# Attention's output products issued in halves of a weight block, each half behind one head's values; the first chunk's first two k tiles with their low-row products last

## The chip, the cores and the metric

The kernel runs on one core of a Trainium2 chip. The metric is device time in microseconds (us) of one execution; the median of several executions is compared. TensorE (PE) does the matmuls, and its weight loads are listed apart as PEld. VectorE (DVE), ScalarE (ACT) and GpSimd (POOL) do the rest, and SyncE (SP) issues most transfers. Each engine works through its own instructions in the order that was fixed when the kernel was built.

## The reference

Two layers over 256 rows of 1024 channels, each of the form half a SwiGLU feed-forward, a mixer, half a second feed-forward. The mixer of layer 0 is a convolution module, that of layer 1 is multi-head latent attention with 8 heads. What the change touches is the end of the attention and the start of a feed-forward:

```python
s = (q_nope . k_nope + q_rope . k_rope) * scale      # per head, 2 blocks of 128 queries, chunk-causal mask
p = softmax(s)
o = p . v                                            # per head, 128 channels
h = h + concat(o over 8 heads) @ w_o                 # (256 x 1024) @ (1024 x 1024)
h = h + 0.5 * (silu(n @ w1) * (n @ w3)) @ w2         # n = RMSNorm(h), w1 and w3 (1024 x 2816)
```

Everything is float32 in the inputs and the output.

## The kernel before, in words

**Three products for one.** A float32 matrix is split in a high part (a cast to fp32r) and a low part (what the cast left). `mm3` (line 271) makes one product of three matmuls into the same PSUM tile: high rows by low weights (the page's line 273), high rows by high weights (276), low rows by high weights (277). The rows' two parts are Xh and Xl for a feed-forward and Oh and Ol for the attention's outputs; the weights' are `hi` and `lo`. `some` (279) makes a chosen subset of the three, named by the letters l, h and x in that order.

**Weights.** The weights come as blocks of 128 x 2048 in a fixed list (`blocks`). `load_to` (209) issues a block's transfer into one of 3 `raw` buffers (SP's queue), casts the high part on ACT (line 187) and subtracts on DVE (line 188), each in 2 pieces, into one of 5 pairs of buffers. `weights` (213) takes the next block for use and calls `load_ahead`. A cast is ordered behind the last 6 urgent instructions of its engine that were written down before it (`behind`, 141).

**The order.** The build (line 1503) has a planner that simulates a timeline and gives every engine a fixed order: of the instructions that its simulation holds ready, the one of the highest priority goes next. Priority is the place in the program, except for functions wrapped in `urgent` (193), which go ahead. `order` (137) adds a constraint between two instructions without a wait of its own. The planner's order can therefore differ from the program's: work written later is pulled forward where the engine would otherwise stand idle in the simulation.

**Attention's heads** (lines 1289 to 1374). For a head, `scores` (1294) makes the two score tiles in one PSUM bank of tag B (of 3), `softmax` (1306) takes the maxima on DVE, the powers on ACT (1315) and the scaling on DVE (1320); `probs` (1324) transposes the three 128 x 128 blocks into another bank of tag B (tp, line 317) and copies them on ACT (1327, `ptT`); `values` (1334) multiplies with V into the only bank of tag C (pv, 1336 and 1337), and `evicted` (1330) writes Oh on ACT (1331) and Ol on DVE (1332). A head's values wait for the bank until the head before has been evicted. Only heads 3 to 6 have an urgent eviction. The loop over i (1358) writes scores of head i, transposes of head i - 2 and values of head i - 3. The scores of heads 0 to 2 and the last projection (nope) stand ahead of it.

**The output products** are kept by `Rows` (563): four accumulators of 128 x 512 (two blocks of 128 rows `tb`, two halves of the channels `d`). A weight block of `wo` covers two heads (k tiles f = 2i and 2i + 1), so `block(i)` (577) issues 4 accumulators x 2 heads x 3 = 24 matmuls. Blocks 0 and 1 are written after the values of heads 3 and 5 (i = 6 and 8, line 1369); `finish` (584) writes blocks 2 and 3, accumulator by accumulator, adds each to h as it completes and starts the next norm: `early` (392) transposes block 0 of the new rows on PE and splits it into Xh and Xl, `begin` (404) turns block 1 on DVE and by transfers through DRAM (ht, hd, hb), and `end` (414) splits that.

**The feed-forward's first chunk** (`first_chunk`, 642) runs in five stretches of k tiles: gate weights on row block 0 (k 0 to 7), up weights on row block 0 (k 0 to 3), gate on row block 1 (k 0 to 7), then the rest. It is used by the two feed-forwards whose second row block is turned by transfers, which are layer 1's: one starts at 459.59 us of the trace and one, behind the attention, at 730.15 us.

Of the kernel before, what the change touches and what calls it, by code (L numbers as in the profile page):

```python
# [19 lines left out]
P = 128  # L20
D = 1024
S = 256
NT = S // P
KT = D // P
# [10 lines left out]
VH = 128  # L35
# [7 lines left out]
PIECES = 2  # L43
# [41 lines left out]
def trunk(ctx: ExitStack, tc: tile.TileContext, x, xt, first, pos, invf, gfin, wdw,  # L85
          f1w13, f1w2, f2w13, f2w2, cw1, cw2, wa, wuq, wukv, wo, wpair, out):
    nc = tc.nc
# [45 lines left out]
    n_used = [0]  # L133
# [3 lines left out]
    def order(ins, first):  # L137
        tc.add_manual_dep(ins.ins, first.name, mybir.DependencyInfo(
            mybir.DependencyClass.NoSync, mybir.DependencyReason.DATA), reason="order")
# [7 lines left out]
    casts = {}  # L147
# [58 lines left out]
    def load_ahead(ahead=W_BUFS - 2):  # L206
        load_to(min(len(blocks), n_used[0] + ahead))
# [5 lines left out]
    def weights(n=1, more=True):  # L213
        out = []
        for _ in range(n):
            n_used[0] += 1
            if more:
                load_ahead()
            else:
                load_ahead(0)  # L220
            out.append(loaded[n_used[0] - 1])
        return out
# [19 lines left out]
    for k in range(KT):  # L242
        c = slice(k % 4 * 512, k % 4 * 512 + 512)
# [27 lines left out]
    def mm3(o, ah, al, bh, bl, start, stop, after=()):  # L271

        mm = nc.tensor.matmul(o, ah, bl, start=start, stop=False)  # L273
        for a in after:
            order(mm, a.ins)
        nc.tensor.matmul(o, ah, bh, start=False, stop=False)  # L276
        return nc.tensor.matmul(o, al, bh, start=False, stop=stop)  # L277

    def some(o, kinds, ah, al, bh, bl, start, stop):

        for n, kind in enumerate(kinds):
            mm = nc.tensor.matmul(o, al if kind == "x" else ah, bl if kind == "l" else bh,  # L282
                                  start=start and n == 0, stop=stop and n == len(kinds) - 1)
        return mm

    def tbs(tb):
        return slice(tb * P, (tb + 1) * P)
# [275 lines left out]
    class Rows:  # L563
# [10 lines left out]
                         f == f1 - 1, [*after, *after_last] if j else after)  # L574
            return mm

        def block(self, i):
            part, = weights()
            for tb in range(NT):
                for d in range(2):  # L580
                    apart = self.last and (tb, d) == (1, 1)
                    self.mm(part, i, tb, d, self.o[tb, d], 0, self.nk - (4 if apart else 0))

        def finish(self, rh, make_next, act):
            nb = self.nk // 2
# [44 lines left out]
    def ffn_in(act, X, make_next, beside):  # L630
# [11 lines left out]
        def first_chunk(X, u):  # L642

            kn = HB // 512
            parts = weights(3, False)
            X.begin()
            parts += weights(1, False)
            for m in range(2):
                for tb in range(NT):
                    u[m, tb] = bank("A", "u")  # L650
            last = None
            for n, (m, tb, ks) in enumerate(((0, 0, range(8)), (1, 0, range(4)), (0, 1, range(8)), (1, 0, range(4, 8)),
                                             (1, 1, range(8)))):
                if n == 2:
                    X.late()
                elif n == 3:
                    load_ahead()
                for k in ks:
                    hi, lo = parts[2 * m + k // kn]
                    c = slice(k % kn * 512, k % kn * 512 + 512)  # L660
                    mm = mm3(u[m, tb], X.xh[:, k, tbs(tb)], X.xl[:, k, tbs(tb)], hi[:, c], lo[:, c], k == 0,
                             k == KT - 1, (last,) if last is not None and k == ks[0] else ())
                last = mm

        for c in range(6):
# [476 lines left out]
    def mla_in(act, X, make_next, cc, sn):  # L1142
# [146 lines left out]
        Oh = act.tile([P, H, S], F32R, tag="Oh", name="Oh")  # L1289
        Ol = act.tile([P, H, S], F32R, tag="CQ", name="Ol")  # L1290

        score_last, maxima, powers, scaled = [], [], [], []

        def scores(hd):
# [29 lines left out]
        def probs(pr):  # L1324
            b = transposed(pr, 0, 3)
            pt = act.tile([P, 3 * P], F32, tag="ptT", name=uid("ptT"), bufs=2)
            nc.scalar.copy(pt, b[:, :3 * P])
            return pt

        def evicted(hd, b):  # L1330
# [3 lines left out]
        def values(hd, pt):  # L1334
            b = bank("C", "pv")
            nc.tensor.matmul(b[:, :S], VV[:, 0, hd * VH:(hd + 1) * VH], pt[:, :S], start=True, stop=False)
            nc.tensor.matmul(b[:, P:S], VV[:, 1, hd * VH:(hd + 1) * VH], pt[:, S:], start=False, stop=True)

            (urgent if hd in (3, 4, 5, 6) else lambda f: f)(evicted)(hd, b)

        pr, pt = {}, {}
        part, = weights(1, False)
        load_ahead(1)

        table = urgent(nc.scalar.activation)(small.tile([P, 1], F32, tag="silu", name="exp"), neghalf, AF.Exp)
        order(table, kept.ins)
# [11 lines left out]
        for i in range(2, H + 3):  # L1358
            if 2 < i < H:
                pr[i] = scores(i)  # L1360
            if i == 6:
                load_ahead(5)
            if i in (3, 4):
                load_ahead(i - 1 + (i == 4))
            if i - 2 < H:
                pt[i - 2] = probs(pr[i - 2])
            if i - 3 in pt:
                values(i - 3, pt[i - 3])
            if i in (6, 8):
                o.block((i - 6) // 2)  # L1370

            if i in (8, 9):
                load_to(n_used[0] + i - 4)
# [141 lines left out]
```

## Time and profile before

| what | us |
|---|---|
| median of 3 runs (lowest to highest) | 919.18 (918.69 to 919.48) |
| the profiled execution | 918.68 |
| its span, first to last instruction | 916.9 |
| PE busy in the span | 908.9 |
| DVE, ACT, POOL busy | 591.1, 492.8, 127.6 |
| granted TensorE clock, mean | 0.999 |

The profile's page gives busy time by engine, then groups of instructions by source line. Beside it there are lists of who waited for whom, groups by tile, sums over stretches of time, and a timeline by engine; in a timeline each row has its start, its length, its engine, its line, the operation, the tiles (out<-in) and how many were merged, and in square brackets the idle time of the engine before it. A PE row's length is longer than the distance to the next start, because matmuls overlap; the distance between two starts is the time that a matmul takes of the engine.

### The profile page before, as it was taken

Reading aid. Unit: us, or ns where it says so; the run is one execution under the profiler, and the core shown is the slowest. Engines: PE = TensorE matmul, PEld = TensorE weight load, DVE = VectorE, ACT = ScalarE, POOL = GpSimd, SP = SyncE. Lnnn points to the kernel's source line nnn. Section 1 sums busy time; section 2 is a strip of 40 time slices with the busy share of each in tenths; the row PEclk is TensorE's granted clock in tenths of the full one; section 3 lists DMA queues with packets and bytes.
Section 4 is the critical chain, followed back from the end, with each engine's and each line's share of the span. In section 5 each row is a group of like instructions: output and inputs, shape, how many; then the busy total and the mean of one; then the engine's idle time right before and its main releaser. Section 6 shows DMA issues by size and latency. Waiting matters only on the chain.

```text
span 916.9 us, 12085 instructions
## 1 busy us (share of the span) xinstructions
PE 908.9 (99%) x4337; PEld 764.6 (83%) x4337; DVE 591.1 (64%) x931; ACT 492.8 (54%) x842; POOL 127.6 (14%) x261
## 2 busy tenths in 40 slices
PE   9999999999999999999999999999999999999997
PEld 7888888898988888888888888888898888888886
DVE  6886764489987666655476665545768676566533
ACT  7654454388877444543364544443677574454422
POOL 1720000079951000000010000001400000000000
PEclk9999999999999999999999999999999999999999
DMA  9987776533227667766567777754445478776711
GB/s 339 321 294 248 277 253 222 188 139 138 93 85 270 243 233 239 251 222 226 184 203 271 260 244 239 239 203 132 168 143 184 149 258 277 250 250 217 252 46 46
DMA packets 65292, 194.73 MB, mean 212 GB/s; under 512 B 11728, under 2 KB 37200, under 8 KB 45904
## 3 DMA queue, kind: packets, MB, share of 16 engines
q1 hardware_dynamic: 64800, 193.28, 60.7%
q8 instruction: 34, 0.56, 0.2%
q10 hardware_dynamic: 432, 0.69, 0.2%
q14 instruction: 26, 0.21, 0.1%
HBM read 179.78 MB, written 14.16 MB: 212 GB/s over the span
## 4 chain that ended last, share of the span: by engine, by line
PE 99%; DMA 0%; ACT 0%; POOLq 0%; DVE 0%; issue 0%; POOL 0%; ACTq 0%
PE u L277 17%; PE u L273 17%; PE u L276 17%; PE o L273 10%; PE o L277 10%; PE o L276 10%; PE u L753 3%; PE gate L753 3%; PE o L988 2%; PE tp L317 1%; PE u L282 1%; PE pairs L796 1%; PE a L273 1%; PE a L277 1%; PE a L276 1%; PE nope L277 1%
## 5 line engine op out<-in xcount | busy, mean ns | idle before, releaser
L188 DVE TENSOR_TENSOR lo<-raw,hi 128x1024 fp32r<-128x1024 f32 (+1 forms) x292 | 344.8, 1220 | 175.9 <-ACT hi L187 174.8
L187 ACT CAST hi<-raw 128x1024 fp32r<-128x1024 f32 x294 | 292.6, 1047 | 240.8 <-PE o L277 85.5
L273 PE MATMUL u<-lo,Xh 128*128 128x512 f32 x688 | 268.0, 389 | 0.0
L276 PE MATMUL u<-hi,Xh 128*128 128x512 f32 x688 | 267.7, 389 | 0.0
L277 PE MATMUL u<-hi,Xl 128*128 128x512 f32 x688 | 267.6, 389 | 0.0
L277 PEld LDWEIGHTS u<-hi,Xl 128*128 128x128 f32 x688 | 129.1, 188 | 27.2 <-DVE Xl L336 0.5
L273 PEld LDWEIGHTS u<-lo,Xh 128*128 128x128 f32 x688 | 129.1, 188 | 27.0 <-DVE lo L188 0.4
L276 PEld LDWEIGHTS u<-hi,Xh 128*128 128x128 f32 x688 | 129.1, 188 | 27.0
L276 PE MATMUL o<-hi,Gh 128*128 128x512 f32 (+1 forms) x356 | 137.9, 387 | 0.0
L277 PE MATMUL o<-hi,Gl 128*128 128x512 f32 (+1 forms) x356 | 137.8, 387 | 0.0
L273 PE MATMUL o<-lo,Gh 128*128 128x512 f32 (+1 forms) x356 | 137.2, 387 | 0.0
L308 POOL TENSOR_TENSOR ms<-ss 128x1 f32<-128x1 f32 x16 | 10.0, 628 | 586.7 <-ACT junk L300 586.7
L277 PEld LDWEIGHTS o<-hi,Gl 128*128 128x128 f32 x356 | 66.9, 188 | 13.5
L273 PEld LDWEIGHTS o<-lo,Gh 128*128 128x128 f32 x356 | 66.9, 188 | 13.5
L276 PEld LDWEIGHTS o<-hi,Gh 128*128 128x128 f32 x356 | 66.9, 188 | 13.4
L640 DVE TENSOR_TENSOR Gl<-gb,Gh 128x512 fp32r<-128x512 f32 (+1 forms) x48 | 31.3, 652 | 56.6 <-ACT Gh L639 56.6
L639 ACT CAST Gh<-gb 128x512 fp32r<-128x512 f32 (+1 forms) x48 | 28.0, 583 | 73.3 <-DMA gb<-gd 73.3
L842 DVE SCALAR_TENSOR_TENSOR acc<-V,dw,acc 128x128 f32<-128x128 f32 (+1 forms) x174 | 53.9, 394 | 0.0
L863 ACT ACTIVATE prod<-V,dw 128x128 f32<-128x128 f32 (+1 forms) x128 | 45.6, 415 | 1.9 <-POOL Y L864 1.0
L715 DVE TENSOR_TENSOR s<-s,u 128x512 f32<-128x512 f32 (+1 forms) x48 | 30.5, 635 | 7.6 <-PE u L277 7.3
L714 ACT ACTIVATE s<-u,R 128x512 f32<-128x512 f32 (+1 forms) x48 | 31.2, 649 | 5.9 <-PE u L277 4.8
L864 POOL TENSOR_TENSOR odd<-odd,prod 128x128 f32<-128x128 f32 (+1 forms) x62 | 33.0, 536 | 0.2
(218 smaller groups left out, 858.1 us busy)
## 6 DMA issues: line engine op xcount, KB each, us to landing
raw<-in_f2w SPq DMA_DIRECT2D x66, 1024.0 KB, 4.9
raw<-in_f1w SPq DMA_DIRECT2D x62, 1024.0 KB, 5.0
raw<-in_cw SPq DMA_DIRECT2D x12, 1024.0 KB, 4.8
gd<-gt SPq DMA_DIRECT2D x160, 64.0 KB, 3.3
gb<-gd SPq DMA_DIRECT2D x40, 256.0 KB, 4.9
raw<-in_wo SPq DMA_DIRECT2D x4, 1024.0 KB, 4.8
raw<-in_wuq SPq DMA_DIRECT2D x3, 1024.0 KB, 4.8
raw<-in_f1w SPq DMA_DIRECT2D x8, 256.0 KB, 4.9
```

What stands on the lines that cost most here:

```text
L187: casts[len(loaded), i] = (nc.scalar.copy(hi[:, c], raw[:, c]), low.tensor_sub(lo[:, c], raw[:, c], hi[:, c].bitcast(F32)))
L188: low.tensor_sub(lo[:, c], raw[:, c], hi[:, c].bitcast(F32)))
L273: mm = nc.tensor.matmul(o, ah, bl, start=start, stop=False)
L276: nc.tensor.matmul(o, ah, bh, start=False, stop=False)
L277: return nc.tensor.matmul(o, al, bh, start=False, stop=stop)
L640: nc.vector.tensor_sub(Gl[:, f, tbs(tb)].rearrange("p t (i q) -> p t i q", q=32), bv, gh.bitcast(F32))
L714: nc.scalar.activation(s[:, :w], u[0, tb][:, :w], AF.Silu, scale=X.r[tb])
L715: nc.vector.tensor_mul(s[:, :w], s[:, :w], u[0, tb][:, w:] if both else u[1, tb])
L753: mm = nc.tensor.matmul(u[:, t], w[:, c], X.x[:, k, t], start=(k == 0), stop=(k == KT - 1))
L842: dve_last.append(nc.vector.scalar_tensor_tensor(out if j == j1 - 1 else y, v, w, y, op0=ALU.mult, op1=ALU.add))
L863: prods_last.append(nc.scalar.activation(p, v, AF.Copy, scale=w))
L864: pool_last.append(nc.gpsimd.tensor_tensor(o, o, p, op=ALU.add))
```

## The change

`block` can now issue the products of one row block alone, and takes instructions that its products are ordered behind. In the attention's loop, blocks 0 and 1 are issued in four halves, at i = 5, 6, 7 and 8, and every product of a half is ordered behind the last values matmul of head i - 3 (heads 2, 3, 4 and 5). The high-part casts of the weight blocks `n_part + 2` and `n_part + 3` (the third and fourth block of `wo`) are ordered behind the copies of the transposed probabilities of heads 3 and 4. The call of `load_ahead` at i = 6 counts one block fewer, since one block more has been taken by then; the blocks loaded are the same.

In `first_chunk` the first stretch issues, for k = 0 and then k = 1, the two products with the rows' high part, then the two products with the rows' low part, and from k = 2 on the three products together as before. Nothing of the computation is added or left out: the same matmuls in another order.

```diff
--- before.py
+++ after.py
@@ -574,12 +574,14 @@
                          f == f1 - 1, [*after, *after_last] if j else after)
             return mm
 
-        def block(self, i):
-            part, = weights()
-            for tb in range(NT):
+        def block(self, i, rows=range(NT), after=()):
+            if rows[0] == 0:
+                self.part, = weights()
+            part = self.part
+            for tb in rows:
                 for d in range(2):
                     apart = self.last and (tb, d) == (1, 1)
-                    self.mm(part, i, tb, d, self.o[tb, d], 0, self.nk - (4 if apart else 0))
+                    self.mm(part, i, tb, d, self.o[tb, d], 0, self.nk - (4 if apart else 0), after=after)
 
         def finish(self, rh, make_next, act):
             nb = self.nk // 2
@@ -648,18 +650,25 @@
             for m in range(2):
                 for tb in range(NT):
                     u[m, tb] = bank("A", "u")
-            last = None
+            last = prev = None
             for n, (m, tb, ks) in enumerate(((0, 0, range(8)), (1, 0, range(4)), (0, 1, range(8)), (1, 0, range(4, 8)),
                                              (1, 1, range(8)))):
                 if n == 2:
                     X.late()
                 elif n == 3:
                     load_ahead()
-                for k in ks:
+                for k, kinds in ([(0, "lh"), (1, "lh"), (0, "x"), (1, "x"), *((k, "") for k in range(2, KT))]
+                                 if n == 0 else [(k, "") for k in ks]):
                     hi, lo = parts[2 * m + k // kn]
                     c = slice(k % kn * 512, k % kn * 512 + 512)
-                    mm = mm3(u[m, tb], X.xh[:, k, tbs(tb)], X.xl[:, k, tbs(tb)], hi[:, c], lo[:, c], k == 0,
-                             k == KT - 1, (last,) if last is not None and k == ks[0] else ())
+                    args = u[m, tb], X.xh[:, k, tbs(tb)], X.xl[:, k, tbs(tb)], hi[:, c], lo[:, c]
+                    if kinds:
+                        mm = some(args[0], kinds, *args[1:], (k, kinds) == (0, "lh"), False)
+                        if prev is not None:
+                            order(mm, prev.ins)
+                        prev = mm
+                    else:
+                        mm = mm3(*args, k == 0, k == KT - 1, (last,) if last is not None and k == ks[0] else ())
                 last = mm
 
         for c in range(6):
@@ -1289,6 +1298,7 @@
         Oh = act.tile([P, H, S], F32R, tag="Oh", name="Oh")
         Ol = act.tile([P, H, S], F32R, tag="CQ", name="Ol")
 
+        turned = []
         score_last, maxima, powers, scaled = [], [], [], []
 
         def scores(hd):
@@ -1324,7 +1334,7 @@
         def probs(pr):
             b = transposed(pr, 0, 3)
             pt = act.tile([P, 3 * P], F32, tag="ptT", name=uid("ptT"), bufs=2)
-            nc.scalar.copy(pt, b[:, :3 * P])
+            turned.append(nc.scalar.copy(pt, b[:, :3 * P]))
             return pt
 
         def evicted(hd, b):
@@ -1334,13 +1344,15 @@
         def values(hd, pt):
             b = bank("C", "pv")
             nc.tensor.matmul(b[:, :S], VV[:, 0, hd * VH:(hd + 1) * VH], pt[:, :S], start=True, stop=False)
-            nc.tensor.matmul(b[:, P:S], VV[:, 1, hd * VH:(hd + 1) * VH], pt[:, S:], start=False, stop=True)
+            mm = nc.tensor.matmul(b[:, P:S], VV[:, 1, hd * VH:(hd + 1) * VH], pt[:, S:], start=False, stop=True)
 
             (urgent if hd in (3, 4, 5, 6) else lambda f: f)(evicted)(hd, b)
+            return mm
 
         pr, pt = {}, {}
         part, = weights(1, False)
         load_ahead(1)
+        n_part = n_used[0]
 
         table = urgent(nc.scalar.activation)(small.tile([P, 1], F32, tag="silu", name="exp"), neghalf, AF.Exp)
         order(table, kept.ins)
@@ -1359,15 +1371,20 @@
             if 2 < i < H:
                 pr[i] = scores(i)
             if i == 6:
-                load_ahead(5)
+                load_ahead(4)
             if i in (3, 4):
                 load_ahead(i - 1 + (i == 4))
             if i - 2 < H:
                 pt[i - 2] = probs(pr[i - 2])
+                if i in (5, 6):
+
+                    for piece in range(PIECES):
+                        order(casts[n_part + i - 3, piece][0], turned[-1].ins)
             if i - 3 in pt:
-                values(i - 3, pt[i - 3])
-            if i in (6, 8):
-                o.block((i - 6) // 2)
+                last = values(i - 3, pt[i - 3])
+            if 5 <= i < 9:
+
+                o.block((i - 5) // 2, (range(0, 1), range(1, 2))[(i - 5) % 2], (last,))
 
             if i in (8, 9):
                 load_to(n_used[0] + i - 4)
```

## The prediction

> **What bounds the kernel now.** I read the page's head, the lists of waits, then the timelines of the attention and of the start of the feed-forward behind it. The page first, then the two waits of TensorE's weight loads that touch the change:
>
> ```profile
> span 916.9 us, 12085 instructions
> PE 908.9 (99%) x4337; PEld 764.6 (83%) x4337; DVE 591.1 (64%) x931; ACT 492.8 (54%) x842; POOL 127.6 (14%) x261
> ```
>
> ```profile
> PEld u L277 <- DVE Xl L336: 0.5, 1, 0.5
> PEld u L273 <- DVE lo L188: 0.4, 1, 0.4
> ```
>
> TensorE is the bound: 99% of the span. The second wait lies at the kernel's own start and isn't touched; the first is at the start of the feed-forward behind the attention. A busy PE isn't yet a dense one, because lengths overlap; what counts is the distance between starts. An undisturbed stretch gives the unit (the first and the last of 46 matmuls, the other layer-1 feed-forward's start):
>
> ```profile
> 459.59 0.40 PE L273 MATMUL u<-lo,Xh 128*128 128x512 f32 x1
> ...
> 469.80 0.39 PE L273 MATMUL u<-lo,Xh 128*128 128x512 f32 x1
> ```
>
> 10.21 us over 45 steps is 0.227 us a product. Now the attention, from the end of the last projection to the third head's values:
>
> ```profile
> 692.76 0.49 PE L317 MATMUL tp<-ident,pr 128*128 128x128 f32 x3
> ...
> 694.73 0.60 PE L1336 MATMUL pv<-ptT,VV 128*128 128x256 f32 x2
> ...
> 695.38 0.39 PE L1299 MATMUL sc<-KN,QN 128*128 128x128 f32 x2
> ...
> 696.70 0.49 PE L317 MATMUL tp<-ident,pr 128*128 128x128 f32 x3
> 696.94 0.48 PE L273 MATMUL o<-lo,Oh 128*128 128x512 f32 x1
> ...
> 698.85 0.59 PE L1336 MATMUL pv<-ptT,VV 128*128 128x256 f32 x2
> ...
> 699.42 0.93 PE L277 MATMUL o<-hi,Ol 128*128 128x512 f32 x3
> ...
> 703.18 0.58 PE L273 MATMUL o<-lo,Oh 128*128 128x512 f32 x1
> 703.61 0.40 PE L276 MATMUL o<-hi,Oh 128*128 128x512 f32 x1
> ...
> 705.59 0.70 PE L1336 MATMUL pv<-ptT,VV 128*128 128x256 f32 x2
> ```
>
> The planner pulled output products of heads 0 and 1 forward (696.94 to 698.85, 699.42 and on, 703.18 and on), far ahead of their place behind head 3's values. Two small stalls show. At 703.18 the step to the next product is 0.43 us, where the same step after another switch from transposes or scores to products is 0.32 (730.15 to 730.47, below). At 705.59 the first values matmuls of head 2 take 0.70 us, where head 1's took 0.59. That is 0.1 us each. What head 2 waited for:
>
> ```profile
> 697.28 0.48 ACT L1327 COPY ptT<-tp 128x384 f32<-128x384 f32 x1 [0.51 <-PE tp L317]
> 698.09 0.37 ACT L1315 ACTIVATE pr<-sc,nm 128x128 f32<-128x128 f32 x1 [0.33 <-DVE nm L1313]
> ...
> 698.89 3.88 ACT L187 CAST hi<-raw 128x1024 fp32r<-128x1024 f32 x4
> 702.67 0.37 ACT L1331 CAST Oh<-pv 128x256 fp32r<-128x256 f32 x1
> 702.94 0.49 ACT L1327 COPY ptT<-tp 128x384 f32<-128x384 f32 x1
> ```
>
> ```profile
> 695.99 0.42 DVE L1332 TENSOR_TENSOR Ol<-pv,Oh 128x256 fp32r<-128x256 f32 x1 [0.56 <-ACT Oh L1331]
> ...
> 702.78 2.35 DVE L188 TENSOR_TENSOR lo<-raw,hi 128x1024 fp32r<-128x1024 f32 x2
> 705.12 0.42 DVE L1332 TENSOR_TENSOR Ol<-pv,Oh 128x256 fp32r<-128x256 f32 x1
> ```
>
> Four casts in a row (3.88 us) stood ahead of head 1's eviction, and the subtractions ahead of its low part, so the one bank for values came free only at 705.54. Last, the start of the feed-forward:
>
> ```profile
> 730.15 0.48 PE L273 MATMUL u<-lo,Xh 128*128 128x512 f32 x1
> 730.47 0.40 PE L276 MATMUL u<-hi,Xh 128*128 128x512 f32 x1
> 730.88 0.50 PE L277 MATMUL u<-hi,Xl 128*128 128x512 f32 x1
> 731.22 0.40 PE L273 MATMUL u<-lo,Xh 128*128 128x512 f32 x1
> ```
>
> ```profile
> 727.49 2.06 DVE L590 TENSOR_TENSOR h<-o,h 128x512 f32<-128x512 f32 x3 [0.79 <-PE o L277]
> 729.59 0.71 DVE L349 STREAM_TRANSPOSE ht<-h 128x512 f32<-128x512 f32 x1
> 730.48 0.61 DVE L336 SCALAR_TENSOR_TENSOR Xl<-tp,G,Xh 128x128 fp32r<-128x128 f32 x2 [0.18 <-ACT Xh L332]
> ```
>
> The first product with the rows' low part starts 0.41 us after the one before and the next 0.34 after that: 0.30 us over two units. DVE had three additions and a transposition back to back just before, since the last products of the accumulators came within 0.7 us of each other.
>
> **The change part by part.** No instruction is added or taken away; 4337 matmuls stay 4337. So the sum has only the stalls that go and those that come.
>
> *Casts behind the copies.* The third and fourth `wo` blocks' high casts, those four at 698.89, go behind the copies of heads 3 and 4. Then head 1's eviction no longer has 3.88 us ahead of it: the two stalls of 0.1 us at 703.18 and 705.59 go. Cost: the casts come later, and the subtractions and the buffers' next transfers with them. Head 4's copy I place near 705 (the first half from 700, see the next part, 2.73 for it, 1.56 for scores and transposes, 0.49 for the copy); 2 casts (3.88 us for 4, so 1.94) and their subtractions (2.35) end by 710, while `finish`, which is the first to use those blocks, starts near 717 (700, four halves of 2.73, three heads of 2.1). It hides with 7 us to spare. The transfers of the next feed-forward's blocks queue on SP behind the freed buffers; they move by up to 3 us, and those blocks are used from 730 on.
>
> *Halves.* A half is 12 products, 12 x 0.227 = 2.73 us, and can't start before the values of head 2, 3, 4 or 5. In the trace of before 20 products stood ahead of head 2's values: eight with the high part of head 0, four with its low part, eight with the high part of head 1, 20 x 0.227 = 4.54 us. They are held back now. The question is whether head 2's values then come 4.54 us earlier or whether TensorE stands idle. Bounds: nothing, and 4.54 us. Per head TensorE needs 695.38 to 696.94 for scores and transposes, 1.56 us, and 698.85 to 699.42 for values, 0.57: 2.1 us. The other engines need less:
>
> ```profile
> L1327 ACT COPY ptT<-tp x8: 478/486/491, 693.4 to 721.2; 128x384 f32<-128x384 f32 x8
> L1331 ACT CAST Oh<-pv x8: 367/372/373, 695.6 to 725.9; 128x256 fp32r<-128x256 f32 x8
> L1332 DVE TENSOR_TENSOR Ol<-pv,Oh x8: 416/425/426, 696.0 to 726.3; 128x256 fp32r<-128x256 f32 x8
> L1312 DVE TENSOR_REDUCE nm<-sc x16: 278/352/416, 685.5 to 710.0; 128x1 f32<-128x128 f32 x8, 128x1 f32<-128x256 f32 x8
> ```
>
> ACT: the powers 698.09 to 698.89, 0.80, and 0.49 and 0.37, together 1.66 us. DVE: two maxima 0.70, Ol 0.43, and the scaling with its small ones at most 0.8 (an estimate: two passes over a head's tiles, neither dearer than an Ol), together 1.9. So without casts in between the heads themselves are TensorE's to pace. Followed row by row: from a head's values to its bank being free are 694.73 to 696.41 (the end of head 0's Ol), 1.68 us. Head 1's values can start at 696.94, where its transposed copy and the bank are there; then scores of head 5 to about 698.8. Transposes of head 3 need head 4's powers, which end at 698.89 in the trace, or 0.3 us later if head 1's eviction slips ahead of them. Head 2's values need the bank: 696.94 + 1.68 = 698.6. So the first half begins at about 700 and TensorE loses 0 to 0.3 us on the way. From there each head's 2.1 us has 2.73 us of products behind it, more than the bank's cycle of 1.68; I take 0.1 us in all for new stalls, near the lower bound, because that is where these rows lie, and keep 4.5 as the upper end.
>
> *The end of the attention.* With all heads evicted by some 720, `finish` can run in program order, one accumulator every 12 products (2.73 us) instead of three within 2 us. So the additions spread, block 0's new rows are transposed early, and the low parts are ready before they are used. The start at 459.59 shows this form: there the low parts are made from 458.83 on, 0.76 us before the first product, and nothing waits.
>
> ```profile
> 458.83 1.12 DVE L336 SCALAR_TENSOR_TENSOR Xl<-tp,G,Xh 128x128 fp32r<-128x128 f32 x4 [1.13 <-ACT Xh L332]
> ```
>
> The 0.30 us at 730.88 goes.
>
> *First chunk.* The two low-row products move from third and sixth place to fifth and sixth: 2 x 0.227 = 0.45 us of grace for the first, none for the second. Where the 0.41 us step is still there, this takes it away too; with the part above it is the same 0.30 us, not a second one. At 459.59 nothing waits, so nothing is won.
>
> *What comes next.* Rows of block 1 reach the same feed-forward by transfers, and its first chunk needs their fifth k tile at 741.44:
>
> ```profile
> 740.77 1.28 ACT L421 ACTIVATE Xh<-hb,G 128x128 fp32r<-128x128 f32 x4 [0.65 <-DMA hb<-hd]
> ```
>
> ```profile
> 741.44 0.39 PE L273 MATMUL u<-lo,Xh 128*128 128x512 f32 x1
> ```
>
> A quarter of 1.28 us after 740.77 is 741.1, so 0.3 us are left before 741.44: about what the stall at 730.88 is worth. If PE arrives 0.30 us earlier and the transfers don't, nothing more than some hundredths is lost; with the additions spread, the turning of block 1 starts earlier as well.
>
> *Sum.* 0.1 + 0.1 + 0.30 go, 0.1 comes: 0.4 us less. The profiled execution took 918.68 (span 916.9 and 1.8 around it), 0.5 below the median of 919.18; so 918.3 for an execution like that one, and **918.8** for the median.
>
> **The rivals.**
>
> *Heads left bare.* The 20 products were pulled forward because the planner held nothing else ready. If the chip agrees, because a cast or a subtraction still stands ahead of an eviction or of a power, TensorE idles up to 4.54 us less what is won: 919.18 + 4.54 - 0.5 = 923.2 at most. It decides, that is goes beyond 0.2% (1.84 us, about what a measurement of this kernel tells from no change), once 2.3 us of idle time come. For it: the planner's choice, and ACT's four casts show how far one low-priority job can push a head. Against it: those casts are what the change moves, and the paces above. The stage as it is, full clock and no idle time:
>
> ```profile
> 692.80:705.60 12.80, 12.80 (x78) 11.14 (x75) 10.16 (x24) 8.81 (x21) 0.00 (x0) 1.00 0.58 207
> ```
>
> DVE has 10.16 of 12.80 us here, which is the engine to watch: the subtractions in it now move some 2 to 5 us on, beside heads 4 and 5. [...]
>
> *Nothing is moved on balance.* The planner may still interleave `finish` as before, and the low rows of the first chunk then come in time, only for block 1's fifth k tile to wait; or new stalls of a few tenths eat what is won: 919.2 and within 0.3 us of it. For it: the 0.3 us of slack at 741.44.
>
> *Late weights.* The fourth `wo` block's casts behind head 4's copy delay the transfers of the feed-forward's first blocks, and its first chunk waits. Against: 7 us and more of room in each step. With 2 us lost, 920.8.
>
> *Faster by more.* Removing over 1.84 us needs stalls that the trace doesn't have; all it shows between 692 and 732 are 0.5 us.
>
> **How the numbers follow.** Forecast 0.66, nothing on balance 0.14, bare heads 0.13 (0.10 of it beyond 1.84 us), late weights 0.04, all of it counted as slower, faster by more 0.03. So faster 0.03, same 0.83, slower 0.14. The likeliest's own range is 918.2 to 919.4. The range of all is 918.0 to 921.0: below it lies hardly more than the last case, above it the larger part of the bare heads, about 0.1 together, and another 0.05 for what runs vary by.
>
> **What would show it.** In the timeline of the changed kernel: no product of Oh before head 2's values; those values near 700 rather than 705.59; groups of 12 products behind the values of heads 2 to 5; TensorE without idle time between 692 and 732; pairs of casts behind the copies of heads 3 and 4; the low parts of block 0's rows written before the feed-forward's first product, and no entry for them in the waits of the weight loads. The prediction is wrong if that list shows tenths of a microsecond for `tp` or `pv` behind DVE or ACT rows in the attention (bare heads), or for `o` or `u` behind casts (late weights).

## The result and the profile after

The changed kernel takes **922.36 us** (median of 7 executions, 921.01 to 922.98) against 918.74 (7 executions, 918.28 to 919.48) for the kernel before on the same chip: a ratio of 1.0034, interval 1.0024 to 1.0044. It is slower: by 0.34% as the ratio has it, by 3.6 us between the medians. The prediction was 918.8 with a range up to 921.0: the time went the other way, and lies above the range. The profiled execution took 921.32, its span is 919.5; before it was 918.68 and 916.9.

The head of the page after, then the waits of TensorE and of its weight loads:

```profile
span 919.5 us, 12088 instructions
PE 909.2 (99%) x4337; PEld 764.6 (83%) x4337; DVE 589.8 (64%) x931; ACT 492.2 (54%) x842; POOL 127.6 (14%) x261
```

```profile
PEld pv L1346 <- DVE Ol L1342: 2.4, 1, 2.4
PEld L265 <- DVE still L260: 1.0, 1, 1.0
PEld o L273 <- DVE s L724: 1.0, 1, 1.0
```

TensorE does the same work in the same busy time (909.2 against 908.9), in a span 2.6 us longer. The list has a wait that the one before didn't have: 2.4 us of `pv` behind `Ol`, one occurrence. (The wait of `o` behind `s` lies near 131 us, in layer 0. The order of the instructions there is the one of before. In another execution of the same kernel, the first experiment below, TensorE loses less at that place, 0.29 us by the distance between starts against 0.74 here; I take its half microsecond for what executions vary by; that is not shown beyond these two.)

TensorE's timeline after, from the end of the last projection to the fifth head's values; columns as in the prediction:

```profile
693.27 0.49 PE L317 MATMUL tp<-ident,pr 128*128 128x128 f32 x3
...
699.83 0.60 PE L1346 MATMUL pv<-ptT,VV 128*128 128x256 f32 x2
...
700.40 0.48 PE L273 MATMUL o<-lo,Oh 128*128 128x512 f32 x1
...
703.03 0.39 PE L277 MATMUL o<-hi,Ol 128*128 128x512 f32 x1
...
706.21 0.59 PE L1346 MATMUL pv<-ptT,VV 128*128 128x256 f32 x2
...
706.78 0.48 PE L273 MATMUL o<-lo,Oh 128*128 128x512 f32 x1
...
709.62 0.91 PE L317 MATMUL tp<-ident,pr 128*128 128x128 f32 x6
712.69 0.70 PE L1346 MATMUL pv<-ptT,VV 128*128 128x256 f32 x2 [2.16 <-DVE Ol L1342]
```

Head 2's values come at 699.83, groups of 12 products follow (700.40 to 703.03, and from 706.78), and both small stalls near 703 and 705 are gone. Then, at 709.62, TensorE makes the transposes of heads 5 and 6 and has nothing more: head 4's values start 3.07 us later. Six transposes take 0.74 between starts (three take 0.33 at 693.27, and the last switch some 0.1 more), so about 2.33 us are lost; the bracket counts 2.16 from the modelled end. ScalarE's timeline of the same stretch, then VectorE's:

```profile
705.52 2.00 ACT L187 CAST hi<-raw 128x1024 fp32r<-128x1024 f32 x2
...
708.22 2.00 ACT L187 CAST hi<-raw 128x1024 fp32r<-128x1024 f32 x2
710.11 0.38 ACT L1341 CAST Oh<-pv 128x256 fp32r<-128x256 f32 x1
```

```profile
709.94 2.35 DVE L188 TENSOR_TENSOR lo<-raw,hi 128x1024 fp32r<-128x1024 f32 x2
712.21 0.42 DVE L1342 TENSOR_TENSOR Ol<-pv,Oh 128x256 fp32r<-128x256 f32 x1
```

The row at 705.52 is the fourth `wo` block, behind head 4's copy as the change asks. The row at 708.22 is the block after it, the first one of the feed-forward behind the attention. Its two casts stand ahead of head 3's eviction (710.11) and its two subtractions, 2.35 us, ahead of head 3's low part (712.21). Head 3's values were complete by about 707.0 (706.64 and 0.38), but their bank came free only at 712.6, and the products that filled such a time before are now ordered behind head 4's values. ScalarE's timeline of before, for the same block and the same eviction:

```profile
707.52 2.01 ACT L187 CAST hi<-raw 128x1024 fp32r<-128x1024 f32 x2
...
711.58 0.37 ACT L1331 CAST Oh<-pv 128x256 fp32r<-128x256 f32 x1 [1.68 <-PE pv L1337]
```

So the block's casts were ahead of head 3's eviction then too, at nearly the same time (707.52, now 708.22), and cost nothing: ScalarE stood idle for 1.68 us behind them, waiting for the values. It is the heads that moved. TensorE's row of before for head 3's values:

```profile
710.73 0.59 PE L1336 MATMUL pv<-ptT,VV 128*128 128x256 f32 x2
```

They start 4.5 us earlier now (706.21), and meet casts that stayed where they were. The change also puts two casts of the third `wo` block, 700.74 to 702.64, ahead of head 2's eviction; there the twelve products behind head 2's values cover the delay.

The start of the feed-forward after, TensorE and then VectorE:

```profile
733.02 0.48 PE L282 MATMUL u<-lo,Xh 128*128 128x512 f32 x1
...
734.03 0.62 PE L282 MATMUL u<-hi,Xl 128*128 128x512 f32 x2
734.49 0.39 PE L273 MATMUL u<-lo,Xh 128*128 128x512 f32 x1
```

```profile
730.36 2.06 DVE L592 TENSOR_TENSOR h<-o,h 128x512 f32<-128x512 f32 x3 [0.79 <-PE o L277]
```

Six products take 734.49 - 733.02 = 1.47 us: 6 x 0.227 = 1.36 and 0.1 for the switch. The stall of 0.30 us is gone, although the three additions still stand back to back, as before.

So, for the profiled executions: the attention takes 733.02 - 693.27 = 39.75 us where it took 730.15 - 692.76 = 37.39, 2.36 more; the chunk gives back 0.30; about half a microsecond is the place near 131. That is 2.56 of the 2.64 us between the two profiled executions.

This leaves the last microsecond. The profiled execution (921.32) is one of the three shorter ones of seven; the other four lie at 922.36 to 922.98. The first experiment shows what they have besides.

### The profile page after: what moved, and what is told of

The parts are those of the page before. It is cut to its first block, busy times and chain, and to the rows that moved or that the text cites. A ratio compares the mean times of both kernels' runs of the same rounds, so it can differ in the third digit from the quotient of the medians.

```text
span 919.5 us, 12088 instructions
## 1 busy us (share of the span) xinstructions
PE 909.2 (99%) x4337; PEld 764.6 (83%) x4337; DVE 589.8 (64%) x931; ACT 492.2 (54%) x842; POOL 127.6 (14%) x261
## 4 chain that ended last, share of the span: by engine, by line
PE 84%; DMA 9%; DVE 3%; ACT 1%; SPq 1%; issue 1%; POOLq 0%; POOL 0%; ACTq 0%; DVEq 0%
PE u L276 13%; PE u L273 13%; PE u L277 13%; PE o L273 9%; PE o L276 9%; PE o L277 9%; DMA raw<-in_f1w 5%; PE u L762 3%; PE gate L762 3%; PE o L997 2%; DMA gb<-gd 2%; DMA gd<-gt 2%; DVE lo L188 2%; PE tp L317 1%; PE pairs L805 1%; ACT hi L187 1%
## 5 line engine op out<-in xcount | busy, mean ns | idle before, releaser
L349 DVE STREAM_TRANSPOSE gt<-s 128x512 f32<-128x512 f32 (+1 forms) x48 | 32.0, 666 | 1.4
```

The source lines that it names most:

```text
L349: nc.vector.transpose(t[:, :w], src.rearrange("p (t j q) -> p j t q", t=n, q=32))
```

## The experiments

My theory after the result: two parts of the change together make the idle time. The products that are held behind a head's values leave TensorE nothing else, and the casts and subtractions of the feed-forward's first block make head 3's eviction late. Rival one: the idle time is the price of holding products back alone, whoever evicts. Rival two: the casts' new place alone costs it. Rival three: the first chunk or the weights behind it lose the time, and the idle time is made up for elsewhere. No kernel here leaves out any of the computation. The kernel before ran beside each group on the same chip, with medians of 919.11 (the changed kernel again, the late load, the halves alone and the first chunk alone), 919.25 (casts alone, the free block and one piece), 919.16 (subtractions, one subtraction, two more) and 918.97 (four and eight more).

**The changed kernel once more**, without an edit.

> The changed kernel as it is. Late eviction (the feed-forward's first block's casts stand ahead of head 3's eviction): the 2.3 us idle time of TensorE before head 4's values is there again, and the time is 2 to 4 us above the kernel before. Elsewhere (part of the excess lies outside the attention, as the 0.9 us of idle time near 130 us in the first profile): that idle time is there again too. If it is chance, it is gone in this profile.

It took 922.03 (921.01 to 923.09, 6 executions), ratio 1.0032, interval 1.0021 to 1.0044. The profiled execution was the longest of them, 923.09. TensorE's timeline in it:

```profile
712.86 0.70 PE L1346 MATMUL pv<-ptT,VV 128*128 128x256 f32 x2 [2.17 <-DVE Ol L1342]
...
714.11 0.63 PE L276 MATMUL o<-hi,Oh 128*128 128x512 f32 x1
714.53 0.63 PE L277 MATMUL o<-hi,Ol 128*128 128x512 f32 x1
...
717.04 0.39 PE L277 MATMUL o<-hi,Ol 128*128 128x512 f32 x1
```

The same idle time, and behind it products 0.42 us apart instead of 0.227. The granted clock is 0.5 from 713.55 to 716.97, 3.413 us, so half of that, 1.7 us, is lost. In the profile of 921.32 the clock stays at 1.00 through the attention and up to 916.1, behind the last products. The 13 executions of both runs fall into two groups, six at 921.01 to 921.43 and seven at 922.36 to 923.09, about 1.5 apart in their medians. The mean granted clock is 0.998 or 0.999 in the six, and 0.996 or 0.997 in six of the seven (the seventh, 922.98, shows 0.999, which I can't explain). So the median of 922.36 is 918.74, plus some 2.3 for the idle time and its small change, plus the clock in a little more than half of the executions.

**The load behind head 3's values.** Head 3's values are written first, so that the feed-forward's first block, whose casts are low in priority and ordered only behind the urgent work written ahead of them, goes behind the eviction. All else of the change stays.

```diff
-            if i == 6:
-                load_ahead(4)
...
                 last = values(i - 3, pt[i - 3])
+                if i == 6:
+                    load_ahead(4)
```

> The changed kernel with the loading of the feed-forward's first block written behind head 3's values instead of ahead of them, so that its casts come after that head's eviction. Late eviction: the idle time goes, and the time is 0 to 0.6 us below the kernel before. Bare heads (the heads' own chain is too long once the products are held back, wherever the casts stand): TensorE still idles 1 us or more in the attention and the time stays 1 to 3 us above before.

918.55 (918.17 to 919.35, 11 executions), ratio 0.9995, interval 0.9986 to 1.0004. The timeline of all engines around the place:

```profile
707.91 0.38 ACT L1341 CAST Oh<-pv 128x256 fp32r<-128x256 f32 x1
708.17 2.02 ACT L187 CAST hi<-raw 128x1024 fp32r<-128x1024 f32 x2
...
709.05 0.41 DVE L1342 TENSOR_TENSOR Ol<-pv,Oh 128x256 fp32r<-128x256 f32 x1
...
709.64 0.60 PE L1346 MATMUL pv<-ptT,VV 128*128 128x256 f32 x2
709.83 2.35 DVE L188 TENSOR_TENSOR lo<-raw,hi 128x1024 fp32r<-128x1024 f32 x2
```

The eviction is ahead of the casts, the low part ahead of the subtractions, and head 4's values start at 709.64 without a wait. The products are held back as in the change, so holding them costs nothing by itself: rival one falls. This kernel's attention runs as the prediction described; its 0.56 us under the kernel before is the size that was predicted (0.4), but the interval reaches over 1. It is the fastest of all, not shown to be faster than before.

**Halves alone.** The first chunk's order and the casts' order are those of before (of the edit, the part on the casts is shown).

```diff
-                if i in (5, 6):
-
-                    for piece in range(PIECES):
-                        order(casts[n_part + i - 3, piece][0], turned[-1].ins)
...
```

> The halves alone: no casts behind copies, first chunk as before. Without that order the planner puts the casts of the third and fourth output block first and the feed-forward's block behind head 3's eviction. Late eviction: no idle time at head 4's values, time within 0.5 us of before. Bare heads: the products are held back all the same, so 1 to 3 us above before.

918.96 (918.20 to 920.17), ratio 1.0000, interval 0.9991 to 1.0008. TensorE has no idle time in the attention: with the `wo` blocks' casts free to go early, the feed-forward's casts come at 708.60, behind head 3's eviction at 707.53, although the load stands in the program where the change has it. The stall at the start of the feed-forward is there as before:

```profile
731.33 0.40 PE L276 MATMUL u<-hi,Xh 128*128 128x512 f32 x1
731.74 0.50 PE L277 MATMUL u<-hi,Xl 128*128 128x512 f32 x1
732.08 0.39 PE L273 MATMUL u<-lo,Xh 128*128 128x512 f32 x1
```

**The first chunk alone.** The attention is that of before; only `first_chunk` has the change (a part of what differs from the changed kernel):

```diff
-                o.block((i - 5) // 2, (range(0, 1), range(1, 2))[(i - 5) % 2], (last,))
...
+                o.block((i - 6) // 2)
...
```

> The first chunk's new order alone. It takes away the 0.30 us before the third product of the feed-forward behind the attention: 0.3 us below before if that is won for good; no change if the second row block's transfers make TensorE wait later on.

918.96 (918.62 to 919.63), ratio 1.0000, interval 0.9991 to 1.0008. The stall of 0.30 is gone, and the list of waits has one that wasn't there:

```profile
PEld u L273 <- ACT Xh L421: 0.2, 1, 0.2
```

That is the weight load for the first product on block 1's rows. The 0.3 us of slack that the prediction read there is used up by the 0.3 us won, and a little is given back: by starts the step behind that product is 0.31 us (741.51 to 741.82), 0.08 over the unit. What is won doesn't show in the median, 0.15 us below before and within the interval. Rival three falls with these two runs: neither part loses the time.

**The casts' order alone.** The products as before, the first chunk as before.

> Kernel before, with only the two casts ordered behind the copies of heads 3 and 4. The feed-forward's casts then stand ahead of head 3's eviction as in the changed kernel, but output products are free to be pulled forward. Late eviction with products held back needs both: here products fill the wait, TensorE idles under 0.5 us and the time is within 0.5 us of before. If the late eviction alone is enough: 1.5 to 2.5 us above before.

919.64 (919.12 to 920.43), ratio 1.0003, interval 0.9994 to 1.0012. Head 3's eviction is late here too, behind four casts and with its low part behind the subtractions (at 713.75), but TensorE has products to go on with and idles some 0.65 us by starts (0.39 in the bracket; under 0.5 was expected). Rival two falls: the casts' order makes the eviction late, and alone it costs 1.1 us at most by the interval, not 3.6.

**The second block not held.** The change with the halves of block 1 free to go ahead of the values.

```diff
-                o.block((i - 5) // 2, (range(0, 1), range(1, 2))[(i - 5) % 2], (last,))
+                o.block((i - 5) // 2, (range(0, 1), range(1, 2))[(i - 5) % 2], (last,) if i < 7 else ())
```

> Changed kernel, but the second block's products are not ordered behind the values of heads 4 and 5. The casts stand ahead of head 3's eviction as in the changed kernel. If the idle time is there because no product is free, head 2's twelve products (2.7 us) can now fill it: under 0.5 us of idle time, time 0 to 0.6 us below before. If the heads' chain itself is late: 1 us or more stays.

918.99 (918.77 to 919.80), ratio 0.9997, interval 0.9988 to 1.0006. The timeline of all engines:

```profile
710.03 2.36 DVE L188 TENSOR_TENSOR lo<-raw,hi 128x1024 fp32r<-128x1024 f32 x2
710.07 0.38 ACT L1341 CAST Oh<-pv 128x256 fp32r<-128x256 f32 x1
...
711.29 0.40 PE L273 MATMUL o<-lo,Oh 128*128 128x512 f32 x1
...
712.30 0.42 DVE L1342 TENSOR_TENSOR Ol<-pv,Oh 128x256 fp32r<-128x256 f32 x1
```

Head 3's low part is as late as in the changed kernel (712.30 against 712.21), and no time is lost, since products of block 1 run meanwhile. With the run before, the late load and the halves alone this settles it: a late eviction and held products each cost nothing that these runs can tell, and together they are 2.33 us.

**One piece behind the eviction.** Of the block's two casts with their subtractions, the second is ordered behind head 3's eviction. `outs` keeps the two instructions of each head's eviction, and an entry of `casts` is one piece's cast and subtraction.

```diff
+                if i == 6:
+                    for cast, out_ in zip(casts[n_part + 4, 1], outs[3]):
+                        order(cast, out_.ins)
```

> Changed kernel, with one of the feed-forward block's two cast pieces (and its subtraction) behind head 3's eviction and one ahead of it. Late eviction: the idle time is cut by one cast or one subtraction, 0.9 to 1.2 us, to 1.1 to 1.4 us, and the time by as much. Bare heads: no change in the idle time.

919.03 (918.40 to 920.97), ratio 1.0000, interval 0.9991 to 1.0009, and 0.1 us of idle time. This was a miss: with one piece ordered, the planner put the other one's subtraction behind the low part as well (low part at 709.50, both subtractions from 710.10), so half of the work didn't cost half of the time. A planner's order doesn't split in proportion.

**Who holds the bank.** Two kernels order only subtractions behind head 3's low part: both of them (below), and the second one alone. The casts stay ahead of the eviction.

```diff
+                if i == 6:
+                    for piece in range(PIECES):
+                        order(casts[n_part + 4, piece][1], outs[3][1].ins)
```

> Changed kernel, with only the subtractions of the feed-forward's first block behind the low part of head 3; its casts stay ahead of head 3's eviction on ACT. If DVE's 2.35 us of subtractions are what TensorE waits for, idle time of 0.5 to 0.8 us is left, which is ACT's share, and the clock stays at full speed: 0 to 0.6 us above before. If ACT's casts are the cause: 2 us of idle time stay.

> As the last, but one of the two subtractions stays ahead of head 3's low part: idle time of 1.2 to 1.5 us. If the time follows the idle time alone: 0.8 to 1.3 us above before. If an idle time of this length can halve the clock, some executions are 1.7 us longer still.

Both behind: 919.31 (918.72 to 919.61), ratio 1.0002, interval 0.9993 to 1.0011. One behind: 919.91 (919.64 to 920.67), ratio 1.0010, interval 1.0001 to 1.0019. Head 4's values in the two timelines, one fence for each:

```profile
710.80 0.70 PE L1348 MATMUL pv<-ptT,VV 128*128 128x256 f32 x2 [0.48 <-DVE Ol L1344]
```

```profile
711.32 0.70 PE L1348 MATMUL pv<-ptT,VV 128*128 128x256 f32 x2 [1.03 <-DVE Ol L1344]
```

By distance between starts the idle time is 0.65 and 1.19 us against 2.33. So of 2.33 the two casts on ScalarE leave 0.65 and the two subtractions on VectorE make the other 1.7. Neither kernel shows a second group of times.

**More idle time.** Two, four and eight subtractions of 128 x 512 go ahead of head 3's low part on VectorE, into a spare tile that nothing reads. The kernel with two:

```diff
...
+                    spare = tmp.tile([P, 512], F32, tag="s", name=uid("spare"))
+                    more = [nc.vector.tensor_sub(spare, VV[:, 0, c:c + 512], VV[:, 1, c:c + 512]) for c in (0, 512)]
+                    order(more[0], casts[n_part + 4, 1][1].ins)
+                    order(more[1], more[0].ins)
+                    order(outs[3][1], more[1].ins)
```

> Changed kernel, with two more subtractions on DVE (128x512 each, into a spare tile that nothing reads) between the feed-forward block's subtractions and head 3's low part: idle time of 3.6 us instead of 2.3. If the clock falls to half after an idle time that fills a window of 3.4 us, it falls in every execution, and the times are in one group near 919.1 + 3.6 + 1.7 = 924.4 less some tenths. If it is only the idle time: 922.4 and one group.

> The changed kernel with four more subtractions of 128x512 (0.66 us each in the run with two) on VectorE ahead of head 3's low part, into a spare tile that nothing reads; nothing of the computation is left out. Idle time of TensorE: 2.33 + 4 x 0.66 = 5.0 us. The changed kernel without the half clock took 921.0 to 921.4, so 923.8 without it and 925.5 with its 1.7 us. If the clock falls by the length of the idle time alone, every execution from here on lies near 925.5, in one group, and the profile shows products 0.43 us apart behind head 4's values. If it falls by chance, as the run with two subtractions (3.65 us of idle time, clock kept in its profiled execution) suggests, some executions stay near 923.8.

> As the kernel with four more subtractions, with eight: idle time 2.33 + 8 x 0.66 = 7.6 us, 926.5 us without the half clock and 928.2 with it. This is over twice the 3.41 us for which the half clock was granted. If what counts is that some fixed stretch of about that length is idle as a whole, wherever it begins, then here none can miss it: the clock falls in every execution and all lie near 928.2. If executions near 926.5 remain, the fall doesn't hang on the length of the idle time in a way that these runs can tell.

Two: 923.77 (922.68 to 925.40, 5 executions), ratio 1.0055, interval 1.0042 to 1.0069. The idle time is 3.65 us, as worked out, but the executions are not one group: the profiled one, 922.68, kept its clock, the others took 0.9 to 2.7 longer. Four: 926.64 (925.71 to 926.82, 4 executions), ratio 1.0079, interval 1.0064 to 1.0094; none near 923.8. Eight: 928.87 (928.60 to 929.29, 4 executions), ratio 1.0106, interval 1.0089 to 1.0123; none near 926.5. In the kernels with four and eight the subtractions delay the scaling of the powers too, so the idle time comes in two pieces, by the brackets 3.45 and 1.22 us with four, 3.45 and 3.87 with eight. In both the clock falls in the profile, and the time is a little over what was expected with it; it stays at half for two and three times 3.413 us, where the expectation had one.

These profiles show where the clock fell. In the execution of 923.09 the half clock lasts 3.413 us; with four and eight subtractions more it lasts twice and three times as long (714.98 to 721.80, 712.49 to 722.73). So I took sums over stretches of that length. A trace shows a border only where the clock changes; the borders ahead of a fall are counted back from it in that length, which is an estimate. Where the attention shows 1.00 throughout, that fall is the one behind the last products (915.64 in the kernel before, 916.10 in the changed kernel, 917.10 with two more). The columns are stretch, length, busy time of PE, PEld, DVE, ACT and POOL with counts, granted clock, DMA share and GB/s. First the changed kernel's execution with full clock, two stretches, and then the one of 923.09 with its fall at 713.55:

```profile
707.89:711.30 3.41, 2.63 (x15) 1.94 (x13) 3.37 (x8) 3.41 (x10) 0.00 (x0) 1.00 0.40 96
711.30:714.71 3.41, 2.02 (x10) 1.75 (x11) 2.38 (x6) 1.13 (x4) 0.00 (x0) 1.00 0.95 360
```

```profile
710.14:713.55 3.41, 1.24 (x10) 0.89 (x8) 3.29 (x7) 1.72 (x7) 0.00 (x0) 1.00 0.81 305
713.55:716.97 3.42, 3.42 (x11) 2.74 (x10) 0.42 (x1) 0.75 (x2) 0.00 (x0) 0.50 0.83 309
```

Then the kernels with two, four and eight subtractions more:

```profile
708.88:712.29 3.41, 1.69 (x11) 1.18 (x9) 3.37 (x7) 2.86 (x8) 0.00 (x0) 1.00 0.51 168
712.29:715.71 3.42, 1.64 (x8) 1.46 (x9) 2.46 (x8) 0.69 (x2) 0.00 (x0) 1.00 0.97 357
```

```profile
711.57:714.98 3.41, 0.61 (x3) 0.34 (x3) 3.38 (x8) 0.00 (x0) 0.00 (x0) 1.00 0.89 351
714.98:718.39 3.41, 2.78 (x8) 2.32 (x9) 1.00 (x3) 0.75 (x2) 0.00 (x0) 0.50 0.39 166
718.39:721.80 3.41, 3.41 (x10) 2.64 (x9) 0.00 (x0) 0.00 (x0) 0.00 (x0) 0.50 0.00 0
```

```profile
709.08:712.49 3.41, 1.51 (x10) 1.03 (x8) 3.38 (x7) 2.67 (x8) 0.00 (x0) 1.00 0.57 178
712.49:715.90 3.41, 0.87 (x3) 0.48 (x3) 3.34 (x8) 0.00 (x0) 0.00 (x0) 0.50 0.94 368
```

TensorE is busy for 1.24 us in the stretch ahead of the fall at 713.55, for 0.61 ahead of the one at 714.98 (four more) and for 1.51 ahead of the one at 712.49 (eight more). The stretches with 2.63 and 2.02 us (the changed kernel) and with 1.69 and 1.64 (two more) were followed by the full clock. At the kernel's end the last products (128x256) run out. Here are the last two stretches at the full clock of the kernel before, then the last one of the kernel with two subtractions more and the one behind it:

```profile
908.81:912.22 3.41, 1.58 (x14) 1.38 (x12) 2.16 (x5) 1.48 (x6) 0.98 (x4) 1.00 0.38 147
912.22:915.64 3.42, 0.00 (x0) 0.00 (x0) 0.62 (x2) 0.72 (x1) 0.28 (x1) 1.00 0.43 153
```

```profile
913.69:917.10 3.41, 0.70 (x6) 0.50 (x5) 1.88 (x5) 1.57 (x5) 1.04 (x3) 1.00 0.13 47
917.10:920.52 3.42, 0.00 (x0) 0.00 (x0) 0.05 (x1) 0.16 (x1) 0.00 (x0) 0.50 0.44 153
```

In the kernel before, the stretch with 1.58 us was followed by the full clock, and the one with none by a fall at 915.64; with two more the fall at 917.10 came behind 0.70 us, and in the changed kernel's profile the fall at 916.10 came behind 0.33 (912.69 to 916.10). These are eleven stretches of six executions, from two places, the attention and the kernel's end. What decides the clock is not shown by them. Back to full it went behind stretches in which TensorE was busy throughout (3.42 us up to 716.97, 3.41 up to 721.80); the one with 2.78 us from 714.98 was followed by another at half.

The length of the idle time alone doesn't settle it: 3.49 us by the bracket kept the clock in the profiled execution with two more (1.69 and 1.64 us busy), and 2.17 us lost it in the one of 923.09 (1.24 us busy). My reading of the two groups of times, an estimate from these rows, is that an idle time of 2.2 us lies in one such stretch in some executions and is cut in two in others, as in the profile of 921.32 (2.63 and 2.02). No run was made to place a border, and only the profiled executions show where the clock changes.

## Why the prediction was wrong, point by point

*The step that failed* is the term for new stalls in *Halves*: "I take 0.1 us in all for new stalls, near the lower bound". It measured 2.33 us, and the clock added 1.7 in the execution of 923.09; by the groups of times it added some 1.5 in 7 of 13. The bounds, nothing and 4.54, held; the place between them was wrong. The paces per head were worked out "without casts in between", and *Casts behind the copies* followed the two `wo` blocks that the diff names and no other. The next block's casts stood at 707.52 in the trace of before, in plain sight of a stretch into which the prediction itself had moved heads 3 and 4. They didn't move with them. A line that the change leaves where it was allows that: the load at i = 6 is written before head 3's values, and its casts are ordered only behind urgent work already written. The casts that the change holds back bring it about: in the halves alone the line stands at the same place, and the planner put the block's casts behind the eviction (708.60 and 707.53).

*Heads left bare*, at 0.13, was what happened, in the words that it had: "a cast or a subtraction still stands ahead of an eviction". Its price (up to 923.2) held, though of what came in the execution of 923.09 1.7 us were the clock's and not in it; its border of 2.3 us was met, and VectorE was "the engine to watch". What spoke against it, "those casts are what the change moves", was true of head 1's eviction only: every job of that kind had to be set against the heads' new times.

*The clock* has no term in the sum. The runs showed what it can cost this kernel: 3.413 us at half clock, 1.7 us lost, behind 2.17 us of idle time in one place (the execution of 923.09). By the groups of times it came in 7 of 13 executions.

*Right:* head 2's values near 700 (699.83); groups of 12 behind heads 2 and 3; the stalls near 703 and 705.59 gone; no late weights; the 0.3 us of slack for block 1's rows as the next thing to wait (the first chunk alone shows it, 0.2). The sum of -0.4 is that of the kernel with the load behind head 3's values: -0.56, within what the runs vary by.

*Right for a wrong reason:* the 0.30 us at the feed-forward's start goes, but not because `finish` runs in program order, as *The end of the attention* had it. The three additions are back to back as before, and the halves alone keep the stall (731.74). The first low part is written at 733.3, behind the first product, and not ahead of it. It is the first chunk's new order that removes the stall, which the prediction held to be the spare remedy.

## What to carry to other kernels

When a change lets a chain of work run earlier, list on every engine that the chain passes the jobs that don't move with it, and set each against the chain's new times: a job that filled idle time before can stand in the way now, as the two casts at 708.22 stood ahead of head 3's eviction (710.11). Work that is held back to keep an order is also the work that hid the other engines' delays (0.65 us of idle time with the products free, in the casts alone, 2.33 with them held); before holding it, look at the longest job that can stand ahead of the release, here two casts and two subtractions, and write the load behind the eviction that must not wait.

## What the runs showed of the hardware

I had not expected that TensorE's clock is half for 3.413 us behind an idle time of 2.17 us (the execution of 923.09), nor that the same program then has two groups of times, about 1.5 us apart. In the six executions above TensorE was busy for 0.00 to 1.51 us of the 3.41 us ahead of a fall, and for 1.58 to 2.63 us in the five stretches that no fall followed. By the brackets of the timeline, an idle time of 1.0 us shows no fall (one subtraction: 1.00 in the profile from 707.25 to 714.07, and one group of times in 11 executions), 2.2 us shows one in 7 of 13 (by two profiles and the groups of times), and 3.45 and 1.22 us close together show one in the profiled execution, with a mean clock of 0.995 or 0.996 in all 4. The mean granted clock told the two groups of the changed kernel apart in 12 of 13 executions: 0.998 or 0.999 in the six shorter ones, 0.996 or 0.997 in six of the seven longer.
